# GpSimd adds the two halves of the softmax sums' accumulator, and TensorE multiplies one half with ones

## The chip, the cores and the metric

The kernel runs on one core of a Trainium2 chip. The metric is the device time of one execution in microseconds (us). Each time is the median of several runs; a profile is taken from one further execution, and its span runs from its first to its last instruction.

## What is computed

One layer of a block for 4096 tokens of width 1024. Of the reference, the part that bears on the change is the softmax of sparse attention: 8 query heads over 2 key heads (4 heads a group), 64 wide, where each query sees up to 256 selected keys in earlier chunks of 64:

```python
s = jnp.einsum('bqgrd,bqkgd->bqgrk', qg, kg).astype(jnp.float32) * scale
s = jnp.where(valid[:, :, None, None, :], s, -jnp.inf)
p = jax.nn.softmax(s, axis=-1).astype(v.dtype)
o = jnp.einsum('bqgrk,bqkgd->bqgrd', p, vg)
```

Before it come an RMS norm and one input projection, and the indexer that selects the keys; behind it the gates, two branch products, their sum and the output projection.

## The kernel before

The kernel has four stages, one after the other: norm and projections, the indexer (which leaves for each query block a row of biases, 0 for a selected key and -1e30 for another), the attention, and the output stage. All of the attention works in float32 or float32r (float32 data in a faster mode of TensorE).

The attention runs over 64 units: 32 blocks b of 128 queries, and for each the two key groups g. The text numbers them 0 to 63 in this order, so unit u has b = u // 2. A unit has b + 1 key tiles (kt) of 128 keys, with keys on the partitions and 4 heads x 128 queries on the free axis. For each key tile:

- TensorE computes the logits into a PSUM tile st: two float32r matmuls of 512 columns (L1306, L1307), the second with a row that subtracts the query's maximum.
- VectorE adds the transposed bias bT and writes one half of an SBUF tile tt (L1310); ScalarE takes the exponential in place (L1313). A tile tt holds two key tiles: even ones in half 0, odd ones in half 1.
- TensorE multiplies the exponentials with the values into pv (L1322, `values`), for up to four key tiles at a time, in full float32. Each matmul stands in the trace as two records.
- GpSimd adds each tt to the accumulator acc, both halves in one instruction of 128x1024 (L1337), or half 0 alone, 128x512, if the unit's last key tile has no partner (L1341).

When a unit's key tiles are done, `sums` multiplies acc with a matrix of ones on TensorE and so adds up its 128 partitions (L1355): for each half r of acc and each pair f of heads one float32 matmul of 256 columns, four in all, so eight records. ScalarE copies the result to sm (L1359), SP writes it to DRAM (sumD), reads it back as rl with queries on the partitions (L1368), VectorE takes the reciprocal (L1369), and SP writes it to invD for the output stage. In the last unit the last four tiles tt are not added to acc; the ones multiply them directly.

Beside this, one or two units ahead, TensorE computes the logits of queries on the partitions into ps (L1267), from which VectorE takes the maxima (L1273); they go through DRAM too (maxD, qm). When the last maxima are done, the SP queue starts loading the output stage's weights (raw), which ScalarE and VectorE split into two float32r parts (wb, wa; L235, L237).

The order of instructions on each engine is written by a planner (`Plan`). Every step has an engine, a cost in us, a key, and the steps that it waits for. The planner plays the program through with these costs (and 2.0 us for a DMA to land), lets each engine start the ready step with the lowest key whose buffers are free, and emits the instructions in the order in which they start. It charges 0.12 us more where TensorE changes between float32r and float32 steps. So a cost that changes can move other steps too. On the chip each engine then runs its list in that order, and waits wherever the next instruction isn't ready. Of the buffers, acc has 2, tt 8, st 3, ps 2.

Of the kernel before, what the change touches and what calls it, by code (L numbers as in the profile page):

```python
# [18 lines left out]
OP = mybir.AluOpType  # L19
# [100 lines left out]
class Plan:  # L120
# [11 lines left out]
    def new(self, name):  # L132
        return Tile_(name)
# [107 lines left out]
class K:  # L241
# [890 lines left out]
    def phase_attention(self):  # L1132
# [17 lines left out]
        v, act, pe, gp = nc.vector, nc.scalar, nc.tensor, nc.gpsimd  # L1150
# [18 lines left out]
        pl = Plan()  # L1169
# [116 lines left out]
        def softmax(u):  # L1286
            b, g = units[u]
# [3 lines left out]
            acc, pv, prev, pvs, T, E, done = new("acc"), new("pv"), None, None, {}, {}, 0  # L1291
            direct = DIR if u == len(units) - 1 else 0
            end = at[u + 1]
            runs = -(-(b + 1) // PVN)
            ends = {-(-(b + 1) * (i + 1) // runs) - 1 for i in range(runs)}
            for kt in range(b + 1):
# [18 lines left out]
                if kt in ends:  # L1315
# [3 lines left out]
                    def values(some=some):  # L1319
                        for k in some:  # L1320
                            for f in range(2):
# [3 lines left out]
                                 use=[pv] + [T[q] for q in range(some[0] // 2, kt // 2 + 1)], form=1)  # L1325
                if r == 0 and kt < b:
                    continue
                if p == 0:
                    prev = E[kt]
# [4 lines left out]
                def add(tt=tt, p=p, r=r):  # L1334
# [3 lines left out]
                    else:  # L1338
                        if p == 1:
                            gp.tensor_copy(acc.t[:, 1], first[:, 1])  # L1340
                        gp.tensor_tensor(acc.t[:, 0], first[:, 0], tt.t[:, 0], op=OP.add)  # L1341
                prev = pl.add("pool", 2.3 if r else 1.23, i, add, [prev, E[kt], E[kt - r], E[0], E[1]],
                              [acc] if p == 1 else [], [tt] + ([T[0]] if p == 1 else [acc]))
            ov = new("ov")
            evac = pl.add("act", 0.27, end, lambda: act.activation(ov.t, pv.t, AF.Copy), [pvs], [ov], [pv])
            ps, sm, rl = new("st"), new("sm"), new("rl")

            terms = [(acc if b >= 2 else T[0], min(b + 1, 2))] + [
                (T[p], min(b + 1 - 2 * p, 2)) for p in range(max(1, b // 2 - direct + 1), b // 2 + 1)]

            def sums():
                mine = [(x, r) for x, n in terms for r in range(n)]
                for x, r in mine:
                    for f in range(2):
# [3 lines left out]
                        use=[ps] + [x for x, _ in terms], form=1)  # L1358
# [22 lines left out]
        for b in range(NB):  # L1381
            base = (at[2 * b - 1] if b else 0) - AL - AP
            while first <= b:
                keys(first, base - (b - first) * 1.5)
                first += 1
            queries(b, base)
            flip(b)
            for u in (2 * b, 2 * b + 1):
                maxima(u)
            done = list(pl.steps)  # L1390
            for u in (2 * b, 2 * b + 1):
                softmax(u)
# [182 lines left out]
```

## Time and profile before

| | |
|---|---|
| median of 3 runs | 4342.46 us (4341.94 to 4343.56) |
| profiled execution, its own time | 4339.42 us |
| its span, first to last instruction | 4337.6 us |
| mean granted TensorE clock, share of full | 0.981 |
| TensorE busy | 4176.9 us (96%) |
| VectorE busy | 3226.5 us (74%) |
| ScalarE busy | 2348.8 us (54%) |
| GpSimd busy | 1823.8 us (42%) |

The shares are averages over four stages with different limits. The attention lies between about 2140 and 3600 us of the span; what the change does is read there. In the rows, PE is TensorE, PEld its weight loads, DVE VectorE, ACT ScalarE, POOL GpSimd, and SPq the queue of the engine that issues the DMAs. A number in square brackets behind an instruction is the time that its engine sat idle before it, and the instruction that ended the wait. A stretch in which matmuls overlap counts once as busy; one matmul's duration is longer than the distance to the next one's start.

### The profile page before, as it was taken

The page shows a single profiled execution, that of the slowest core. Times are in us where ns is not written, and L with a number is a line of the kernel's source. Part 1 is how long each engine was busy: PE and PEld are TensorE (multiplying, and loading weights), DVE is VectorE, ACT ScalarE, POOL GpSimd, SP SyncE. Part 2 cuts the span into 40 slices and gives each one's busy share as a digit, 9 for nine tenths or more (in the row PEclk, how much of TensorE's full clock was granted, in tenths as well). Part 3 has the DMA queues.
Part 4 walks back from the last instruction along what each step waited for, and adds up shares of the span by engine and source line. Part 5 has one row for each costly group of instructions (what it writes and reads, how often), then busy time and mean ns, then how long its engine had stood idle before and what let it go on. Part 6 is the DMA issues. An engine that isn't in the chain of part 4 may idle for free. (4 is left out here: it accounts for less than half of the span.)

```text
span 4337.6 us, 77494 instructions
## 1 busy us (share of the span) xinstructions
PE 4176.9 (96%) x27986; PEld 3517.3 (81%) x27987; DVE 3226.5 (74%) x7858; ACT 2348.8 (54%) x3993; POOL 1823.8 (42%) x1657
## 2 busy tenths in 40 slices
PE   8999899999999999999789999999999997999999
PEld 7988899999998999999556666666666656999998
DVE  6545688888989888787578889999999995434342
ACT  5444687777777887886445455555555552111110
POOL 3555222223224332010146678888888881111111
PEclk9999999999999999999799999999999998999999
DMA  6666545545445446666432212212211116444442
GB/s 226 249 235 241 185 161 174 175 173 182 164 166 179 154 159 219 213 220 219 135 65 55 59 44 48 47 47 52 43 38 38 24 27 188 154 135 149 140 141 83
DMA packets 461118, 586.39 MB, mean 135 GB/s; under 512 B 165885, under 2 KB 358969, under 8 KB 456506
## 3 DMA queue, kind: packets, MB, share of 16 engines
q1 hardware_dynamic: 460730, 581.40, 41.4%
q8 instruction: 221, 3.62, 0.4%
q14 instruction: 167, 1.37, 0.1%
HBM read 388.54 MB, written 175.54 MB: 130 GB/s over the span
## 5 line engine op out<-in xcount | busy, mean ns | idle before, releaser
L1043 PE MATMUL pd<-h,wgh 128*128 128x256 f32 x3584 | 1020.4, 285 | 9.7 <-ACT row L417 8.3
L1044 PE MATMUL pd<-h,wgh 128*128 128x256 f32 x3584 | 1013.6, 283 | 0.0
L1045 PE MATMUL pd<-h,wgl 128*128 128x256 f32 x3584 | 1012.7, 283 | 0.0
L1337 POOL TENSOR_TENSOR acc<-acc,tt 128x1024 f32<-128x1024 f32 x388 | 925.7, 2386 | 143.7 <-ACT tt L1313 122.7
L1313 ACT ACTIVATE tt<-tt 128x512 f32<-128x512 f32 x1056 | 653.1, 631 | 601.6 <-DVE tt L1310 599.4
L1310 DVE TENSOR_TENSOR tt<-st,bT 128x512 f32<-128x512 f32 x1056 | 693.8, 684 | 82.5 <-PE st L1307 75.5
L1043 PEld LDWEIGHTS pd<-h,wgh 128*128 128x128 f32 x3584 | 682.1, 190 | 28.2 <-ACT row L417 8.6
L761 DVE SCALAR_TENSOR_TENSOR ring<-rl,wi,ring 128x1024 f32<-128x1024 f32 (+7 forms) x624 | 689.9, 1148 | 12.8 <-ACT rl L759 10.3
L1044 PEld LDWEIGHTS pd<-h,wgh 128*128 128x128 f32 x3584 | 682.9, 191 | 14.9 <-DMA h<-hD 0.2
L1273 DVE CUSTOM_DVE_ANT_0 jk<-ps,bias 128x1024 bf16<-128x1024 f32 (+7 forms) x640 | 655.9, 1028 | 40.2 <-PE ps L1267 39.5
L1045 PEld LDWEIGHTS pd<-h,wgl 128*128 128x128 f32 x3584 | 682.9, 191 | 0.0
L759 ACT ACTIVATE rl<-ps 128x1024 f32<-128x1024 f32 (+7 forms) x624 | 539.4, 889 | 134.2 <-PE ps L756 61.1
L1322 PE MATMUL pv<-tt,vv 128*64 128x256 f32 x4224 | 529.9, 392 | 0.0
L846 ACT ACTIVATE sg<-ring,tk 128x2048 fp8e4<-128x2048 f32 (+7 forms) x322 | 485.4, 1509 | 38.5 <-DVE tk L833 21.2
L1306 PE MATMUL st<-qa,kk 128*128 128x512 f32 x1056 | 455.9, 432 | 18.4 <-DVE tt L1310 18.2
L1322 PEld LDWEIGHTS pv<-tt,vv 128*64 128x64 f32 x4224 | 281.5, 138 | 212.4 <-issue 79.8
L1307 PE MATMUL st<-qm,kl 65*128 65x512 f32 x1056 | 421.6, 399 | 1.1 <-DMA qm<-maxD 1.1
L1267 PE MATMUL ps<-kk,qa 128*128 128x512 f32 (+3 forms) x1152 | 362.7, 391 | 13.7 <-DVE mx L1273 13.7
L1505 POOL TENSOR_TENSOR ga<-ga,gb 128x256 f32<-128x256 f32 x128 | 102.1, 803 | 637.9 <-DVE gb L1500 388.3
L756 PE MATMUL ps<-kis,qT 128*128 128x512 f32 (+3 forms) x1136 | 335.4, 382 | 13.6 <-ACT rl L759 13.4
L1437 ACT ACTIVATE yh<-ga 128x256 fp32r<-128x256 f32 x128 | 53.5, 418 | 517.5 <-PE po L1473 314.2
L1306 PEld LDWEIGHTS st<-qa,kk 128*128 128x128 f32 x1056 | 200.6, 190 | 163.0 <-DVE tt L1310 64.1
(321 smaller groups left out, 7777.4 us busy)
## 6 DMA issues: line engine op xcount, KB each, us to landing
h<-hD SPq DMA_DIRECT2D x192, 1024.0 KB
hlD<-rhl SPq DMA_DIRECT2D x32, 1280.0 KB
gD<-sgm SPq DMA_DIRECT2D x256, 128.0 KB
x<-x SPq DMA_DIRECT2D x32, 512.0 KB
wraw<-w_in SPq DMA_DIRECT2D x32, 512.0 KB
hD<-hh SPq DMA_DIRECT2D x32, 512.0 KB
hD<-hl SPq DMA_DIRECT2D x32, 512.0 KB
q<-hlD SPq DMA_DIRECT2D x32, 512.0 KB
```

Of the source, the lines that this page charges most:

```text
L759: r = pl.add("act", 0.05 + n * 0.834e-3, k_, lambda ps=ps, rl=rl, n=n: act.activation(rl.t[:, :n], ps.t[:, :n], AF.Relu), [m], use=[ps, rl])
L761: prev[o] = pl.add("dve", 0.1 + n * 1.04e-3, k_, lambda rl=rl, o=o, n=n, h=h: v.scalar_tensor_tensor(acc[:, o:o + n], rl.t[:, :n], self.wi ...
L846: mine.append(pl.add("act", 0.28 + m * 0.834e-3, key, lambda sg=sg, o=o, m=m, e=e, j=j, b=b: act.activation(sg.t[:, o:o + m], where[b][:, ...
L1043: pe.matmul(out, wh.t[:, k], r1, start=(k == 0), stop=False)
L1044: pe.matmul(out, wh.t[:, k], r2, start=False, stop=False)
L1045: pe.matmul(out, wl.t[:, k], r1, start=False, stop=(k == KT - 1))
L1273: v.tensor_tensor_reduce(out=jk.t[:, :n], in0=ps.t[:, :n], in1=BI[b][0].t[:, o:o + n], scale=1.0, scalar=-3e38, op0=OP.add, op1=OP.max, ac ...
L1306: pe.matmul(s.t, kk[:, g, o], qa.t[:, hs], start=True, stop=False)
L1310: ad = pl.add("dve", 0.602, i, lambda s=s, tt=tt, r=r, kt=kt: v.tensor_tensor(tt.t[:, r], s.t, bc(bt.t[:, kt:kt + 1], [P, 4, P]), op=OP.ad ...
L1313: E[kt] = pl.add("act", 0.52, i, lambda tt=tt, r=r: act.activation(tt.t[:, r], tt.t[:, r], AF.Exp), [ad], use=[tt])
L1322: pe.matmul(pv.t[64 * f:64 * f + 64], vv[:, k, 64 * g:64 * g + 64], T[k // 2].t[:, k % 2, 2 * f:2 * f + 2], start=(k == 0), stop=(k == b))
L1337: gp.tensor_tensor(acc.t, first, tt.t, op=OP.add)
```

## The change

Each unit with b of 2 or more gets one more GpSimd instruction behind its last add: half 1 of acc is added to half 0, in place (128x512, planned at 1.28 us). The ones then multiply half 0 alone, so `sums` has two matmuls (four records) instead of four. Its planned cost falls by 0.43 us through the count of terms, and it waits for the new add. In the last unit the directly multiplied tiles stay as they were.

```diff
             evac = pl.add("act", 0.27, end, lambda: act.activation(ov.t, pv.t, AF.Copy), [pvs], [ov], [pv])
             ps, sm, rl = new("st"), new("sm"), new("rl")
-
-            terms = [(acc if b >= 2 else T[0], min(b + 1, 2))] + [
+            if b >= 2:
+                prev = pl.add("pool", 1.28, end - 1, lambda: gp.tensor_tensor(
+                    acc.t[:, 0], acc.t[:, 0], acc.t[:, 1], op=OP.add), [prev], use=[acc])
+
+            terms = [(acc, 1) if b >= 2 else (T[0], b + 1)] + [
                 (T[p], min(b + 1 - 2 * p, 2)) for p in range(max(1, b // 2 - direct + 1), b // 2 + 1)]
```

Lines behind this place are three higher in the changed kernel: the ones' line L1355 is L1358 there, the reciprocal's L1369 is L1372, and the new add is L1348.

The planner's order changes as well. Numbers behind a name only tell tiles apart. The first place is GpSimd's list at the end of unit 60 (b = 30, an odd number of key tiles), first before, then after the change.

```order
L1337 TENSOR_TENSOR acc_41140<-acc_41140,tt_41434 128x1024
L1341 TENSOR_TENSOR acc_41140<-acc_41140,tt_41457 128x512
L1337 TENSOR_TENSOR acc_41515<-tt_41475,tt_41495 128x1024
L1337 TENSOR_TENSOR acc_41515<-acc_41515,tt_41519 128x1024
...
L1337 TENSOR_TENSOR acc_41084<-acc_41084,tt_41378 128x1024
L1341 TENSOR_TENSOR acc_41084<-acc_41084,tt_41401 128x512
L1348 TENSOR_TENSOR acc_41084<-acc_41084 128x512
L1337 TENSOR_TENSOR acc_41458<-tt_41419,tt_41439 128x1024
L1337 TENSOR_TENSOR acc_41458<-acc_41458,tt_41467 128x1024
```

The new add (L1348) stands between the unit's last add and the next unit's first.

In the same unit TensorE's list keeps its order, but for the number of ones. On VectorE the reciprocal of this unit's sums moves, counted from the adds of the next unit's logits (L1310): before, then after.

```order
L1310 TENSOR_TENSOR tt_41549<-st_41539,bT_40370 128x512
L1273 ISA jk_41564,mx_41358<-ps_41542,bias_40623 128x1024
L1273 ISA mx_41358 128x1
L1310 TENSOR_TENSOR tt_41571<-st_41546,bT_40370 128x512
L1369 RECIPROCAL rl_41551<-rl_41551 128x4
L1310 TENSOR_TENSOR tt_41571<-st_41568,bT_40370 128x512
...
L1310 TENSOR_TENSOR tt_41492<-st_41481,bT_40320 128x512
L1273 ISA jk_41507,mx_41302<-ps_41485,bias_40569 128x1024
L1273 ISA mx_41302 128x1
L1372 RECIPROCAL rl_41494<-rl_41494 128x4
L1310 TENSOR_TENSOR tt_41515<-st_41489,bT_40320 128x512
L1310 TENSOR_TENSOR tt_41515<-st_41511,bT_40320 128x512
```

The reciprocal now stands one logits add earlier.

The third place is TensorE's list around the sums of unit 47 (b = 23), before and after.

```order
L1267 MATMUL ps_37077<-kk,qa_36542 128x512 x2
L1322 MATMUL pv_36860<-tt_37009,vv 64x256 x4
L1322 MATMUL pv_36860<-tt_37037,vv 64x256 x4
L1355 MATMUL st_37096<-acc_36820,ones 64x256 x4
L1306 MATMUL st_37106<-qa_36542,kk 128x512
...
L1322 MATMUL pv_36810<-tt_36969,vv 64x256 x4
L1322 MATMUL pv_36810<-tt_36999,vv 64x256 x4
L1267 MATMUL ps_37049<-kk,qa_36499 128x512 x2
L1306 MATMUL st_37055<-qa_36499,kk 128x512
L1307 MATMUL st_37055<-qm_36500,kl 128x512
L1267 MATMUL ps_37063<-kk,qa_36499 128x512 x2
L1358 MATMUL st_37068<-acc_36780,ones 64x256 x2
L1306 MATMUL st_37073<-qa_36499,kk 128x512
```

Before, the ones follow the values' matmuls in one group of float32 work; now six float32r matmuls stand between, and the ones are a group of their own. Over the whole attention the float32 groups are 297 before and 308 now.

## Rows read from the trace of the kernel before

**Rows 1.** The page's slices: TensorE's busy share in tenths, 40 slices.

```profile
PE   8999899999999999999789999999999997999999
```

**Rows 2.** Busy times by stretch: us, PE, PEld, DVE, ACT, POOL, clock, DMA.

```profile
2140.00:2500.00 360.00, 335.99 (x1925) 214.79 (x1924) 279.42 (x585) 180.59 (x338) 199.79 (x91) 0.95 0.29 62
2500.00:3526.00 1026.00, 1024.39 (x6062) 682.12 (x6061) 959.10 (x1777) 550.18 (x955) 862.53 (x371) 1.00 0.18 40
3526.00:3605.00 79.00, 53.63 (x320) 30.05 (x319) 54.49 (x77) 38.64 (x80) 41.54 (x18) 0.87 0.25 67
```

**Rows 3.** The chain of waits at unit 60's sums: start us, us, what.

```profile
3464.88 0.86 PE st L1355 x8
```

**Rows 4.** Timeline of TensorE, unit 62: start us, us, what.

```profile
3507.64 1.95 PE L1322 MATMUL pv<-tt,vv 128*64 128x256 f32 x16
...
3510.10 0.64 PE L1267 MATMUL ps<-kk,qa 128*128 128x512 f32 x2
...
3512.22 0.39 PE L1307 MATMUL st<-qm,kl 65*128 65x512 f32 x1
3512.54 1.95 PE L1322 MATMUL pv<-tt,vv 128*64 128x256 f32 x16
```

**Rows 5.** Timeline behind the sums of units 15, 47 and 61.

```profile
2281.48 1.29 DVE L1310 TENSOR_TENSOR tt<-st,bT 128x512 f32<-128x512 f32 x2 [0.48 <-PE st L1307]
...
2999.17 1.03 PE L1355 MATMUL st<-acc,ones 128*64 128x256 f32 x8
3000.14 0.50 PE L1306 MATMUL st<-qa,kk 128*128 128x512 f32 x1
3000.43 2.41 POOL L1337 TENSOR_TENSOR acc<-tt,tt 128x1024 f32<-128x1024 f32 x1 [2.33 <-ACT tt L1313]
3000.97 0.69 DVE L1310 TENSOR_TENSOR tt<-st,bT 128x512 f32<-128x512 f32 x1 [1.28 <-PE st L1307]
...
3505.41 0.69 DVE L1310 TENSOR_TENSOR tt<-st,bT 128x512 f32<-128x512 f32 x1 [0.67 <-PE st L1307]
```

**Rows 6.** GpSimd's half adds (ns min/median/max), and the timeline at units 32 and 61.

```profile
L1341 POOL TENSOR_TENSOR acc<-acc,tt x28: 1272/1289/1295, 2189.1 to 3500.0; 128x512 f32<-128x512 f32 x28
...
2591.17 1.29 POOL L1341 TENSOR_TENSOR acc<-acc,tt 128x512 f32<-128x512 f32 x1
2593.37 1.03 PE L1355 MATMUL st<-acc,ones 128*64 128x256 f32 x8
...
3464.28 2.37 POOL L1337 TENSOR_TENSOR acc<-tt,tt 128x1024 f32<-128x1024 f32 x1 [1.08 <-ACT tt L1313]
```

**Rows 7.** Instructions of lines L1310 and L237: ns min/median/max, first and last start.

```profile
L1310 DVE TENSOR_TENSOR tt<-st,bT x1056: 653/685/694, 2127.2 to 3581.0; 128x512 f32<-128x512 f32 x176
L237 DVE TENSOR_TENSOR wb<-raw,wb x16: 407/1416/2564, 3538.4 to 3574.1; 128x256 fp32r<-128x256 f32 x16
L237 DVE TENSOR_TENSOR wa<-raw,wa x16: 411/425/426, 3579.2 to 3601.6; 128x256 fp32r<-128x256 f32 x16
```

**Rows 8.** Loads of rl and reciprocals (units 29, 60); VectorE's waits, 2500 to 3526.

```profile
2533.88 0.34 SPq L1368 DMA_DIRECT2D rl<-sumD  x1
2535.49 0.18 DVE L1369 RECIPROCAL rl<-rl 128x4 f32<-128x4 f32 x1 [1.26 <-DMA rl<-sumD]
...
3468.28 0.34 SPq L1368 DMA_DIRECT2D rl<-sumD  x1
3471.14 0.17 DVE L1369 RECIPROCAL rl<-rl 128x4 f32<-128x4 f32 x1
...
DVE rl L1369 <- DMA rl<-sumD: 5.0, 6, 1.3
```

**Rows 9.** Timeline of TensorE and SP's queue at the attention's end.

```profile
3584.33 3.62 PE L1355 MATMUL st<-tt,ones 128*64 128x256 f32 x32
3595.62 3.67 SPq L229 DMA_DIRECT2D raw<-w_branch_a  x6
3600.02 0.89 SPq L1449 DMA_DIRECT2D o<-bD  x2
```

## The prediction

> **What bounds the kernel now.** I read the page's slices first: the change acts in slices 20 to 34 of 40, from about 2140 to 3600 us, and TensorE is full in most of them [rows 1]. Next the busy times of stretches, with the granted clock, which is at the upper of its two levels (2.4 GHz) in the middle one [rows 2]. From 2500 to 3526 us, the main stretch, TensorE is busy for 1024.39 of 1026 us, VectorE for 959.10 and GpSimd for 862.53: TensorE sets the pace, with VectorE 6% behind. From 2140 to 2500 TensorE is idle for 24 us, waiting for short units' round trips through DRAM. From 3526 to 3605 it works for 53.63 of 79 us: there the SP queue brings in the branch weights, its last copies start at 3595.62, and only behind them, at 3600.02, does it fetch the output stage's first input, while TensorE has begun its last sums at 3584.33 [rows 9].
>
> Busy time counts overlapping matmuls, so what one takes must be read from starts. The chain of waits puts eight ones records, one unit's sums, at 0.86 us [rows 3]: four take 0.43, and sixteen of the values' matmuls, which have the same shape, 1.72. One cycle of 4.90 us, from the pv group at 3507.64 to the next, holds twelve 512-column float32r matmuls (nine of them, from 3510.10 to 3512.22, take 2.12 us, 0.2356 each: 2.83) and the 1.72 [rows 4]. The 0.35 us that are left are the price of going into a float32 group and out of it.
>
> **What the change removes.** Sixty units (numbers 4 to 63 of 0 to 63, b from 2) go from eight ones records to four: 0.43 us of TensorE each, 25.8 in all. That this time is on the path I read at unit 47 [rows 5]: its sums hold TensorE from 2999.17 to 3000.14, VectorE runs dry and waits 1.28 us for the next logits. The same wait stands 1.7 to 2.0 us behind the start of the sums in each of the 47 units from number 15 (0.48 us) to 61 (0.67), and in 42 of them it is over 0.43 us. So VectorE, which is nearly full, is free just where TensorE gets faster. I count the 34 units of the main stretch (28 to 61) in full: -14.6 us. Of the 24 before 2500 I take three quarters, since round trips hold TensorE up for 7% of that stretch and will take some of the gain back: 24 x 0.43 x 0.75 = -7.7 (bounds 0 and -10.3). The last two units count nothing: the weights' copies end later [rows 9].
>
> **What it adds.** GpSimd gets 60 adds of 128x512. An add of that shape and in place stands in the trace 28 times, at 1.289 us (1.272 to 1.295) [rows 6]: 77 us on an engine that is 16% idle in the main stretch. It goes in behind a unit's last add, where GpSimd waits for the next unit's exponentials anyway: 2.33 us ahead of unit 48 [rows 5], 1.08 ahead of unit 61 [rows 6], and about that at the least in the main stretch. The sums, in order in TensorE's queue with the next unit's logits behind them, must now wait for it. In unit 32 the last add starts at 2591.17, ends 1.29 later and the sums start at 2593.37: 0.91 us between them, less than the new add [rows 6]. But the planner counts 1.28 for the add and moves such sums behind other work (as in unit 47, shown with the change). Where the order stays, the spare time is about 1.4 us or more. Cost: 0; without that cover, up to 0.4 us in a unit.
>
> **What it moves.** By the two orders the float32 groups go from 297 to 308, since sums that shared a group with values now often stand alone: 11 x 0.35 = +3.8 us (bounds 0 and 3.8, as some may stand where TensorE waits anyway). The second move is on VectorE. The reciprocal waits there in order for the sums' round trip through DRAM, and everything behind it waits too. In unit 60 the load of rl is issued at 3468.28 and the reciprocal starts at 3471.14, 2.86 us later, without waiting; the quickest that I find from issue to a reciprocal that did wait is 1.61 us (2533.88 to 2535.49) [rows 8]. The planner now puts the reciprocal one logits add earlier in 12 of the 34 units, counted from the sums, and one later in two. Two adds take 1.29 [rows 5], so the 2.86 us become 2.2: between no wait and 0.6 us each on VectorE, 0 to 7 us. VectorE has idle time behind the sums to make it up, so I take +1.
>
> At the end two more adds of 1.29 us run beside the weights' subtractions. The trace shows what that costs: subtractions with both inputs in SBUF take 1.416 us in the median beside GpSimd's adds (wb, up to 2.564) and 0.425 once these have ended (wa), while the logits' add, which reads PSUM and SBUF, lies between 0.653 and 0.694 throughout [rows 7]. I take +1.3 us (bounds 0 and 2.6, the two adds' whole length). The Trainium skill (SBUF — State Buffer, the section on SBUF's two separate sides) says that VectorE and GpSimd share one port pair, that an instruction holds it to its end, and that a VectorE instruction with two SBUF inputs contends for it. The trace agrees, with 1.416 against 0.425. Read without that condition, as any VectorE instruction against any of GpSimd, the rule would speak against this change in every unit (case 5).
>
> **Sum.** -14.6 - 7.7 + 3.8 + 1.0 + 1.3 = -16.2 us against the profiled execution's own 4339.42: 4323.2. The median of the runs shown is 4342.46, 3.0 above; there it makes 4326.
>
> **The rivals.** (1) The forecast, 4318 to 4333.8: 0.66. (2) All of it: every unit gives its 0.43 us and the new groups cost nothing: 4342.46 - 25.8 = 4317. For it speaks that TensorE is busy to 99.8% of the main stretch; against it that 24 us of waits before 2500 have other causes. 0.10. (3) A wait takes the place of the work removed: VectorE is only 6% behind, and the reciprocals stall it. With 7 us of stalls handed on in full, none of the early units' gain and +2.6 at the end: -14.6 + 3.8 + 7 + 2.6 = -1.2, so 4341; with half the early gain 4337. Against it: the six such waits in the main stretch come to 5.0 us now, and TensorE stays full there [rows 2, 8]. 0.13. (4) Slower: TensorE waits at the sums for the added add. With the whole 1.29 us in sixty units it is +77 - 25.8, so 4394; it decides from a mean wait of 0.27 us in a unit, where 60 x 0.27 equals the sum above. For it: the spare time in unit 32 is shorter than the add. Against it: the planner's price for it is within 0.01 us of the trace's, so it moves what would wait. 0.05. (5) Slower too: GpSimd's adds hold up VectorE's logits adds and maxima by their whole length, +77 less 16: 4403. The 0.694 at most, beside an engine that is 84% busy, speaks against it [rows 2, 7]. 0.02. (6) The sums aren't on the path and nothing changes: 4342. Only the last two units look like that. 0.04.
>
> **The numbers.** A measurement of this kernel can tell about 0.2%, 8.7 us. Faster, under 4333.8: cases 1 and 2 and a little of 3, 0.77. The same, up to 4351: the rest of 3, and 6, 0.16. Slower: 4 and 5, 0.07. The range leaves out the tip of case 2 below (0.05) and, above, 4, 5, 6 and the end of 3 (0.14): 4317 to 4340. The likeliest case's own is 4318 to 4333.8.
>
> **What the profile will show.** If it is right: half of the ones records that read acc, 60 more GpSimd adds at 1.29 us, and VectorE's wait behind the sums shorter by 0.43 in most units, so that the main stretch loses some 12 us and the output stage keeps its length. If case 3: waits of the reciprocal for rl well above 5.0 us in the main stretch, and a TensorE that idles in it. If case 4: the sums' line waits for GpSimd's new line. If the early units, in their new order, lose more in round trips than their 7.7, I am wrong on the slower side.

## The result, and the profile after

The changed kernel takes 4315.05 us (4314.77 to 4317.85, four runs) against 4343.01 (4341.94 to 4343.73, four runs): 28.0 us less, a ratio of 0.9938 [0.9925, 0.9951]. The forecast was 16.2 us less, 4326, with a range down to 4317; the time lies 2 us below the range. So the direction was right, and the gain is larger than the sum by 12 us.

The profiled execution took 4317.85 us. The page's slices of TensorE, one digit for each fortieth of the span, answer to [rows 1]:

```profile
PE   8999899999999999999789999999999997999999
```

The busy times by stretch answer to [rows 2] (us, PE, PEld, DVE, ACT, POOL, clock, DMA share, GB/s):

```profile
2140.00:2500.00 360.00, 331.08 (x1880) 211.40 (x1879) 287.01 (x597) 184.87 (x346) 237.88 (x119) 0.96 0.29 62
2500.00:3500.00 1000.00, 998.62 (x5845) 661.13 (x5844) 945.75 (x1756) 541.50 (x942) 893.46 (x398) 1.00 0.18 42
3500.00:3605.00 105.00, 80.19 (x473) 53.41 (x472) 71.17 (x112) 48.52 (x97) 53.44 (x26) 0.85 0.35 99
```

TensorE is full in the main stretch as before (998.62 of 1000), and GpSimd has gone from 84% to 89% of it. In the first stretch TensorE is idle for 29 us in this execution, where it was 24: work went, and waits did not.

The ones, by line, and below them what TensorE's weight loads waited for there (us, times):

```profile
L1358 PE MATMUL st<-acc,ones x240: 379/379/631, 2165.3 to 3560.5; 128*64 128x256 f32 x120
...
  POOL acc L1348: 1.8, 6
```

The new add, and the time that the reciprocals waited for rl over the whole attention, before and after (us, times):

```profile
L1348 POOL TENSOR_TENSOR acc<-acc x60: 1262/1281/1337, 2158.0 to 3551.6; 128x512 f32<-128x512 f32 x60
```

```profile
  DMA rl<-sumD: 51.8, 29
...
  DMA rl<-sumD: 53.9, 27
```

The ones records that read acc are 240, where they were 480; the 60 adds take 1.281 us each, and the sums wait for them in six places, 1.8 us together. Unit 60 shows both, and the wait behind the sums (start us, us, what, idle before):

```profile
3441.82 1.29 POOL L1341 TENSOR_TENSOR acc<-acc,tt 128x512 f32<-128x512 f32 x1
...
3443.18 1.28 POOL L1348 TENSOR_TENSOR acc<-acc 128x512 f32<-128x512 f32 x1
...
3444.42 2.37 POOL L1337 TENSOR_TENSOR acc<-tt,tt 128x1024 f32<-128x1024 f32 x1
...
3444.62 0.60 PE L1358 MATMUL st<-acc,ones 128*64 128x256 f32 x4
3445.15 0.50 PE L1306 MATMUL st<-qa,kk 128*128 128x512 f32 x1
...
3445.91 0.69 DVE L1310 TENSOR_TENSOR tt<-st,bT 128x512 f32<-128x512 f32 x1 [0.72 <-PE st L1307]
```

From the sums' start to the next logits it is 0.53 us. In the trace before, the same two instructions start 0.97 us apart in this unit, and VectorE's wait behind them was 1.17 us, not 0.72:

```profile
3464.71 1.03 PE L1355 MATMUL st<-acc,ones 128*64 128x256 f32 x8
3465.68 0.51 PE L1306 MATMUL st<-qa,kk 128*128 128x512 f32 x1
...
3466.45 0.69 DVE L1310 TENSOR_TENSOR tt<-st,bT 128x512 f32<-128x512 f32 x1 [1.17 <-PE st L1307]
```

Between the sums of units 28 and 61 VectorE's waits fall, for the logits from 40.5 us (first row, before) to 32.5 and for rl from 5.0 [rows 8] to 3.2 (us in total, times, longest):

```profile
DVE tt L1310 <- PE st L1307: 40.5, 70, 2.1
...
DVE tt L1310 <- PE st L1307: 32.5, 67, 1.3
DVE rl L1372 <- DMA rl<-sumD: 3.2, 3, 1.6
```

Where the time went, read from four starts on the way: TensorE's first ps, the sums of units 28 and 61, and the fetch of the output stage's first input. Before (the fetch, at 3600.02, stands in [rows 9]), then after:

```profile
2115.37 0.65 PE L1267 MATMUL ps<-kk,qa 128*128 128x128 f32 x2
...
2507.08 1.03 PE L1355 MATMUL st<-acc,ones 128*64 128x256 f32 x8
...
3503.66 1.03 PE L1355 MATMUL st<-acc,ones 128*64 128x256 f32 x8
...
2113.40 0.65 PE L1267 MATMUL ps<-kk,qa 128*128 128x128 f32 x2
...
2498.04 0.60 PE L1358 MATMUL st<-acc,ones 128*64 128x256 f32 x4
...
3483.13 0.60 PE L1358 MATMUL st<-acc,ones 128*64 128x256 f32 x4
...
3575.73 0.89 SPq L1452 DMA_DIRECT2D o<-bD  x2
```

So the early stretch (first ps to unit 28's sums) is 384.6 us long, where it was 391.7; the main one (to unit 61's sums) 985.1 for 996.6; the tail (to the fetch) 92.6 for 96.4; and the output stage 740.4 for 737.6. That is -7.1, -11.5, -3.8 and +2.8, and with the 2.0 us that the attention began sooner, -21.6, the difference of the two profiled executions. Another execution of the same program (below) has 376.9 in the early stretch, 7.7 us less; 4.7 of that lies between the sums of units 2 and 3, where the change adds and removes nothing (b = 1). This stretch scatters by several us, and the profiled execution here is the slowest of the four.

### The profile page after: what moved, and what is told of

It reads as the page before. It is cut to its first block, busy times and chain, and to the rows that moved or that the text cites. A ratio compares the mean times of both kernels' runs of the same rounds, so it can differ in the third digit from the quotient of the medians.

```text
span 4316.1 us, 77051 instructions
## 1 busy us (share of the span) xinstructions
PE 4154.3 (96%) x27746; PEld 3497.2 (81%) x27747; DVE 3223.0 (75%) x7858; ACT 2347.8 (54%) x3993; POOL 1904.1 (44%) x1717
## 5 line engine op out<-in xcount | busy, mean ns | idle before, releaser
L1337 POOL TENSOR_TENSOR acc<-acc,tt 128x1024 f32<-128x1024 f32 x388 | 925.5, 2385 | 114.0 <-ACT tt L1313 92.5
L1310 DVE TENSOR_TENSOR tt<-st,bT 128x512 f32<-128x512 f32 x1056 | 694.0, 685 | 65.8 <-PE st L1307 60.0
L1306 PE MATMUL st<-qa,kk 128*128 128x512 f32 x1056 | 456.2, 432 | 15.9 <-DVE tt L1310 14.6
L756 PE MATMUL ps<-kis,qT 128*128 128x512 f32 (+3 forms) x1136 | 335.1, 382 | 13.3 <-ACT rl L759 13.2
```

The lines of the kernel that those rows point to most:

```text
L1306: pe.matmul(s.t, kk[:, g, o], qa.t[:, hs], start=True, stop=False)
L1310: ad = pl.add("dve", 0.602, i, lambda s=s, tt=tt, r=r, kt=kt: v.tensor_tensor(tt.t[:, r], s.t, bc(bt.t[:, kt:kt + 1], [P, 4, P]), op=OP.ad ...
L1337: gp.tensor_tensor(acc.t, first, tt.t, op=OP.add)
```

## The experiments

The theory that I started from after the result: the removed work gives about what the sum says, and the rest comes from the planner's new order, which the prediction had counted as a cost only. The rivals: the first profile misled and the time is nearer the forecast; the work alone gives all of it; GpSimd's add costs something that the waits don't show.

Times are medians, with the lowest and highest. Differences are against the kernel before in the same batch (4339.45 for the first four, 4338.71 for the next four, 4339.63 for the last four; its own single runs spread from 4329.45 to 4347.94).

| run | us | ratio [95%] | difference |
|---|---|---|---|
| e1_after_again | 4312.91 (4310.01 to 4313.69) | 0.9935 [0.9921, 0.9948] | -26.5 |
| e2_work_only | 4316.30 (4311.79 to 4319.45) | 0.9942 [0.9929, 0.9956] | -23.2 |
| e3_order_only | 4326.59 (4325.59 to 4329.48) | 0.9970 [0.9957, 0.9982] | -12.9 |
| e4_no_add | 4315.72 (4311.58 to 4318.48) | 0.9942 [0.9928, 0.9955] | -23.7 |
| e5_cost_26 | 4330.62 (4326.35 to 4333.14) | 0.9983 [0.9974, 0.9992] | -8.1 |
| e6_before_fe6 | 4323.09 (4321.20 to 4324.94) | 0.9964 [0.9950, 0.9977] | -15.6 |
| e7_after_fe6 | 4297.24 (4293.25 to 4298.30) | 0.9901 [0.9886, 0.9916] | -41.5 |
| e8_after_land3 | 4297.56 (4296.35 to 4299.14) | 0.9906 [0.9891, 0.9921] | -41.2 |
| e9_order_early | 4331.41 (4322.72 to 4334.17) | 0.9979 [0.9970, 0.9988] | -8.2 |
| e10_order_main | 4341.62 (4337.20 to 4350.12) | 1.0004 [0.9994, 1.0013] | +2.0 |
| e11_order_tail | 4337.18 (4333.63 to 4343.30) | 0.9992 [0.9983, 1.0001] | -2.5 |
| e12_land3_fe6 | 4307.17 (4304.75 to 4311.43) | 0.9923 [0.9910, 0.9937] | -32.5 |

The stretches of each run's profile, cut at the same four starts, with TensorE's idle time in the early one (its length less TensorE's busy time in it):

| run | early | idle in it | main | tail | output stage |
|---|---|---|---|---|---|
| before | 391.7 | 27.5 | 996.6 | 96.4 | 737.6 |
| after | 384.6 | 33.4 | 985.1 | 92.6 | 740.4 |
| e1 | 376.9 | 27.8 | 985.1 | 93.9 | 741.5 |
| e2 work only | 382.4 | 29.1 | 984.1 | 94.1 | 741.0 |
| e3 order only | 379.2 | 19.2 | 1001.4 | 92.6 | 735.5 |
| e4 no add | 380.6 | 28.6 | 982.7 | 96.3 | 743.3 |
| e5 | 379.5 | 24.1 | 996.9 | 95.4 | 738.1 |
| e6 | 376.8 | 18.2 | 996.0 | 96.2 | 739.0 |
| e7 | 365.6 | 19.3 | 985.5 | 92.5 | 738.7 |
| e8 | 360.0 | 16.2 | 984.2 | 90.5 | 747.2 |
| e9 | 378.4 | 20.1 | 997.3 | 95.2 | 740.0 |
| e10 | 391.4 | 27.9 | 998.5 | 95.1 | 738.6 |
| e11 | 392.6 | 30.3 | 998.6 | 95.3 | 735.9 |
| e12 | 365.6 | 19.6 | 984.5 | 90.5 | 747.3 |

**The changed kernel again (e1).** Nothing is edited.

> The changed kernel once more, unaltered, to see how much of its gain repeats. If single executions scatter and the first measurement was lucky, the gain falls to 22 us or less, as the two profiles show (4339.42 and 4317.85, 21.6 apart). If the gain is a property of the kernel, it stays at 28 us, within 2.

It came to -26.5 us: the gain stands in another batch, and is some 10 us over the sum. The rival that the first measurement misled falls. By the table this profile lies 14.8 us under the one of before in the early stretch, 11.5 in the main one and 2.5 in the tail, and 3.9 over it in the output stage.

**The work without the order (e2).** The new add is planned at no cost and the sums at their old one, so that each engine's list is that of before, but for the 60 adds and the halved ones:

```diff
-                prev = pl.add("pool", 1.28, end - 1, lambda: gp.tensor_tensor(
+                prev = pl.add("pool", 0.0, end - 1, lambda: gp.tensor_tensor(
...
-            s1 = pl.add("pe", 0.43 * sum(n for _, n in terms), end + FD, sums, [prev, E[b], pvs],
+            s1 = pl.add("pe", 0.43 * (sum(n for _, n in terms) + (b >= 2)), end + FD, sums, [prev, E[b], pvs],
```

> The work of the change in the order of the kernel before: the added GpSimd instruction and the two ones matmuls that are left are issued, but the planner is told a cost of 0 for the add and the old cost of the sums, so that every engine's list stands as before but for these. Theory A (the work on TensorE is what counts, and the new order costs 3.8 us for its 11 groups and 1 for the reciprocals): -14.6 - 7.7 + 1.3 = -21 us, or -25 if the early units give all of theirs, so faster than the changed kernel's forecast by some 5. Theory B (the new order gave what the forecast lacked): less than 20 us, clearly slower than the changed kernel. If the add makes TensorE wait where the order no longer makes room for it (unit 32 by 0.4, some others by 0.1 to 0.3), 1 to 3 us less.

It gave -23.2 of the 25.8 us that the removed work comes to, so it lies where theory A put it and speaks against B. Between the sums of units 28 and 61 it takes off 12.5 us; 0.43 for each of the 33 units there would be 14.2. The sums do wait for the add in this order, as this row of their line shows (us, times):

```profile
  POOL acc L1348: 8.2, 15
```

With the planner's order it is 1.8 in six places. So the planner's move of the sums does what the prediction said of it, though these 8.2 us are mostly bought back elsewhere, as e4 shows.

**The order without the work (e3).** The other half: before's instructions, in the order that the planner makes with the new costs. A step that emits nothing stands in for the add.

```diff
+            if b >= 2:
+                prev = pl.add("pool", 1.28, end - 1, lambda: None, [prev], use=[acc])
...
-            s1 = pl.add("pe", 0.43 * sum(n for _, n in terms), end + FD, sums, [prev, E[b], pvs],
+            s1 = pl.add("pe", 0.43 * (sum(n for _, n in terms) - (b >= 2)), end + FD, sums, [prev, E[b], pvs],
```

> The order of the changed kernel with the work of the one before: all four ones matmuls and no added GpSimd instruction, but planned as if there were one, and two. Theory A: +3.8 for the 11 new float32 groups and +1 for the reciprocals: 3 to 6 us slower than before. Theory B: faster than before by 5 us or more, by the order alone.

The order alone is worth -12.9 us, as theory B has it, where the prediction had it as a cost. Its profile puts the gain in the early stretch (379.2 for 391.7, with 8.3 us less idle time on TensorE) and in the tail (92.6 for 96.4), and a loss in the main one (1001.4 for 996.6). The two halves make 36.1 us together, and the whole change 26.5 in this batch, so some 10 us are claimed by both. Single places show it: from the sums of unit 21 to those of unit 22 the work alone takes off 3.3 us, the order alone 2.7, and both together 2.6 and 2.7 in the two executions of the changed kernel; from unit 26 to 27 it is 2.6, 6.2 and, together, 6.7.

In the main stretch the changed kernel and e3 have the same order, and there the changed kernel is faster by 0.35 to 0.48 us in 31 of the 33 distances from one unit's sums to the next. So the 0.43 us are on TensorE's path there, unit by unit, as the prediction said. Of the 4.8 us by which e3 is longer than before, 3.2 stand at one place, from unit 29 to 30, where a reciprocal waits 2.73 us for rl; in the other three profiles with this order there (after, e1, e10) it waits 1.35 to 1.60, and the distance is longer by 0.2 at the most. The other 32 distances come to +1.6.

**The work without the add (e4).** As e2, but GpSimd adds nothing; the odd key tiles' exponentials are missing from the sums (a constant of 1e-6 keeps them above zero).

```diff
-            if b >= 2:
-                prev = pl.add("pool", 1.28, end - 1, lambda: gp.tensor_tensor(
-                    acc.t[:, 0], acc.t[:, 0], acc.t[:, 1], op=OP.add), [prev], use=[acc])
```

> The order of the kernel before, the ones matmuls for the even half only, and no added GpSimd instruction: the odd key tiles are left out of the sums (a constant of 1e-6 is added where ScalarE copies them, so that the reciprocal is of something). Against the run with the work in the old order it prices the add alone. Theory A: the add costs 1.3 us at the end and nothing else, so the two agree within 2. Rival: the add costs by making TensorE wait for the sums or by holding up VectorE: then this one is faster by over 4 us.

The time is 0.6 us under e2's, less than either's spread: theory A. Sixty adds, 77 us of GpSimd, cost TensorE nothing that can be told, though in e2 the sums wait for them 15 times; in the main stretch it is 1.4 us (984.1 and 982.7).

**One swap in SP's list (e5).** Set beside e3's, the trace of before loses most at two places, units 12 and 26, some 6 us at each (5.7 from unit 12's sums to the next, 6.2 from unit 26's); I took the second. There SP issues (start us, us, what), in the kernel before, and VectorE and TensorE follow:

```profile
2460.41 0.58 SPq L1281 DMA_DIRECT2D maxD<-mf  x1
2461.04 0.59 SPq L1366 DMA_DIRECT2D sumD<-sm  x2
2463.53 0.68 SPq L1282 DMA_DIRECT2D qm<-maxD  x1
2464.32 1.18 SPq L1368 DMA_DIRECT2D rl<-sumD  x1
...
2468.07 0.18 DVE L1369 RECIPROCAL rl<-rl 128x4 f32<-128x4 f32 x1 [3.79 <-DMA rl<-sumD]
2468.88 0.80 PE L1306 MATMUL st<-qa,kk 128*128 128x512 f32 x1 [3.28 <-DVE tt L1310]
```

The store of another unit's maxima (maxD) stands ahead of that of the sums, and their load (qm), which must wait for it to land, ahead of the load of rl. VectorE, in order, stands still at the reciprocal for 3.79 us, and TensorE, out of logits tiles that VectorE has emptied, for 3.28. The four microseconds of that wait and the twelve behind it, in stretches of 4 us (columns as in [rows 2]):

```profile
2464.00:2468.00 4.00, 1.59 (x10) 1.20 (x8) 0.27 (x1) 0.63 (x1) 1.96 (x1) 1.00 0.09 1
2468.00:2472.00 4.00, 3.12 (x12) 2.33 (x14) 3.94 (x7) 1.71 (x5) 2.37 (x1) 0.54 0.23 44
2472.00:2476.00 4.00, 4.00 (x21) 2.30 (x18) 0.81 (x3) 1.93 (x5) 2.29 (x2) 0.61 0.07 22
2476.00:2480.00 4.00, 4.00 (x26) 2.49 (x25) 3.93 (x7) 2.98 (x6) 2.17 (x2) 1.00 0.61 158
```

Behind the idle time the granted clock is near the lower of its two levels (1.2 GHz, 0.50 of full) for most of 8 us. By these rows that costs another 3.0 us, as an estimate, each busy time multiplied by what the clock lacks of full: 3.12 x 0.46 + 4.00 x 0.39. With the 3.28 it makes 6.3 for one late load. To test this place by itself I changed only the planned cost of unit 26's sums in the kernel before; it swaps SP's stores and loads there:

```diff
-            s1 = pl.add("pe", 0.43 * sum(n for _, n in terms), end + FD, sums, [prev, E[b], pvs],
+            s1 = pl.add("pe", 0.43 * (sum(n for _, n in terms) - (u in (26,))), end + FD, sums, [prev, E[b], pvs],
```

> The kernel before, with one planned number changed: the sums of unit 26 are planned at 0.43 us instead of 0.86. All the work stays. In the SP queue this moves unit 26's store of the sums ahead of the maxima's store, and its load of rl ahead of the load of qm, as the changed kernel's order does; elsewhere a handful of instructions near that place trade places. Theory C (the new order gained where it moved the sums' round trip ahead of the maxima's in the SP queue, so that the reciprocal no longer holds up VectorE): 4 to 7 us faster by this one swap, and VectorE's wait of 3.79 us at unit 26's reciprocal is gone. Rival (the gain of the order came from TensorE's list): 0, within 2.

SP's list and the reciprocal at that place in e5:

```profile
2455.95 0.74 SPq L1366 DMA_DIRECT2D sumD<-sm  x2
2456.73 0.35 SPq L1281 DMA_DIRECT2D maxD<-mf  x1
2457.59 1.09 SPq L1368 DMA_DIRECT2D rl<-sumD  x1
2459.36 0.68 SPq L1282 DMA_DIRECT2D qm<-maxD  x1
...
2460.05 0.18 DVE L1369 RECIPROCAL rl<-rl 128x4 f32<-128x4 f32 x1 [0.28 <-DMA rl<-sumD]
```

The wait of 3.79 us is 0.28, and the same two stretches of 4 us are granted the full clock:

```profile
2459.50:2463.50 4.00, 4.00 (x26) 2.60 (x24) 3.72 (x8) 2.85 (x6) 3.86 (x2) 1.00 0.22 7
2463.50:2467.50 4.00, 4.00 (x26) 3.09 (x26) 3.45 (x7) 3.10 (x7) 2.90 (x2) 1.00 0.60 169
```

The sums of units 26 and 27 start 19.00 us apart (2453.39 and 2472.39), where it was 25.23 (2457.90 and 2483.13): -6.2, as the estimate has it, and the next pair gives another 2.1. The time falls by 8.1 us [0.9974, 0.9992], a little over the 4 to 7 expected. VectorE's reciprocals stand where they stood. One pair of DMAs in another order, with no work removed, is worth about a third of the change. The changed kernel's list has the same order there, and its two sums stand 18.56 apart (2454.74 and 2473.30).

**The other place, unit 12.** No run changes this place alone, but the traces show that it is another case. First before, then e3, behind sums that start at 2238.95 and 2239.00:

```profile
2246.01 1.17 SPq L1368 DMA_DIRECT2D rl<-sumD  x1
2250.19 0.18 DVE L1369 RECIPROCAL rl<-rl 128x4 f32<-128x4 f32 x1 [4.69 <-DMA rl<-sumD]
2251.20 0.47 PE L1267 MATMUL ps<-kk,qa 128*128 128x128 f32 x1 [3.75 <-DVE mx L1273]
...
2247.77 0.52 SPq L1370 DMA_DIRECT2D rl<-sumD  x1
2250.41 0.18 DVE L1371 RECIPROCAL rl<-rl 128x4 f32<-128x4 f32 x1 [2.88 <-DMA rl<-sumD]
2251.82 0.73 PE L1267 MATMUL ps<-kk,qa 128*128 128x512 f32 x2 [1.27 <-DVE mx L1273]
```

The sums' store and load stand behind the maxima's in both, and in e3 the load of rl is issued even later; the reciprocal starts as late, 11.4 us behind the sums for 11.2. But on VectorE it stands two logits adds later, so that VectorE and TensorE have more to do meanwhile. The granted clock from 2248 to 2256 is 0.73 and 0.50 in the two stretches of 4 us before, and 1.00 in e3. e6, below, moves this reciprocal by the same two adds with the same four transfers in the same order on SP, and gains 6.0 us there.

**Later reciprocals (e6, e7).** `FE` is the number of key tiles by which a reciprocal's key lies behind its unit's other late steps. Six for two gives the round trip more time ahead of VectorE's next wait, in the kernel before (e6) and in the changed one (e7):

```diff
-FE = 2
+FE = 6
```

> The kernel before, with the reciprocal planned 6 key tiles behind its sums instead of 2; the SP queue and TensorE keep their order but for a few places. Theory C: VectorE's 51 us of waits for rl mostly go, and with them the part of the early units' stalls that they cause: 5 to 15 us faster. Rival (VectorE's waits for rl cost nothing, as it has idle time): 0, within 2.

> The changed kernel with the reciprocal planned 6 key tiles behind its sums. Theory C: VectorE's waits for rl, 53 us in the changed kernel, mostly go, and it gets 5 to 12 us faster than the changed kernel, so 32 to 40 faster than before. Rival: no difference to the changed kernel.

e6 takes 15.6 us off the kernel before, nearly all of it in the early stretch (376.8 for 391.7). VectorE's waits for rl fall less than I had thought, from 51.8 us over the attention to the first of these rows, e6's; the second is e7's, for 53.9 in the changed kernel.

```profile
  DMA rl<-sumD: 39.4, 20
```

```profile
  DMA rl<-sumD: 27.7, 15
```

TensorE's idle time in the early stretch falls by 9.3 us in e6, to 18.2. From e6 to e7 the change is worth 25.9 us, much as without the later reciprocals (26.5 in e1), and these are worth 15.6 and 15.0: these two gains add. e7, at -41.5, is a little faster than the 32 to 40 expected. That 25.9 is 60 x 0.43 = 25.8 is partly chance: the early stretch gives 11.2 of it (376.8 to 365.6), where the work of 24 units is 10.3, the main one 10.5, where 33 are 14.2, and the tail 3.7, where the prediction counted nothing. No run has the work alone with the later reciprocals, so how much of the 25.9 is order isn't shown.

**A longer landing in the plan (e8, e12).** The planner counts 2.0 us for a DMA to land; here 3.0, in the attention of the changed kernel. In e12 `FE` is 6 as well.

```diff
-                    d.ready = max(d.ready, now + (2.0 if s.eng == "dma" else lat if d.eng != s.eng else 0.0))
+                    d.ready = max(d.ready, now + (self.land if s.eng == "dma" else lat if d.eng != s.eng else 0.0))
...
         pl = Plan()
+        pl.land = 3.0
```

> The changed kernel, planned with 3.0 us instead of 2.0 from a DMA's issue to its landing in the attention; the trace shows 1.6 to 3.9 for the loads of rl. Theory C: the planner then moves the reciprocals and the loads of qm to where they don't wait, in all round trips: 5 to 12 us faster than the changed kernel. Rival: the order only changes by chance, and the time by less than 4 either way.

> The changed kernel with both repairs of the plan: 3.0 us for a DMA's landing, and the reciprocal 6 key tiles behind its sums. If each takes away the same waits: no faster than either alone, some 41 us under the kernel before. If each reaches waits that the other leaves (27 and 16 us of VectorE's waits for rl remain in the two): 3 to 8 us more.

e8 is as fast as e7, by the same stretch (360.0), and beats the 5 to 12 expected. Together they are worse than either, by 9 us, which neither expectation had: of e8's gain in the early stretch 5.6 us are lost, and 3.1 lie ahead of the attention, where no edit reaches. Both runs with 3.0 have an output stage of 747 us, some 4 us or more above all others; their traces put it in its first 75 us, where TensorE is busy for 54 us at a granted clock of 0.80 and 0.78, for 61 at 0.85 in the trace before. What causes that was not tried. e7 and e8 are the best versions here, some 15 us under the changed kernel of e1 by their differences in their own batches.

**The order by parts (e9 to e11).** As e3, but with the new costs for some units alone: 4 to 27 (e9), 28 to 61 (e10), 62 and 63 (e11). Of e9, for the others alike:

```diff
+            if 2 <= b and u < 28:
+                prev = pl.add("pool", 1.28, end - 1, lambda: None, [prev], use=[acc])
...
-            s1 = pl.add("pe", 0.43 * sum(n for _, n in terms), end + FD, sums, [prev, E[b], pvs],
+            s1 = pl.add("pe", 0.43 * (sum(n for _, n in terms) - (2 <= b and u < 28)), end + FD, sums, [prev, E[b], pvs],
```

> The work of the kernel before; only units 4 to 27 are planned as in the changed kernel (the add at 1.28 us that is never issued, the sums at 0.43), so that the order changes in the early stretch alone. Theory C (the order gains through the round trips of the short units): 9 to 13 us faster, with unit 28's sums that much earlier. Rival (the order gains elsewhere, or evenly): under 5 us.

> The same for units 28 to 61 alone: 9 more float32 groups on TensorE (306 for 297), the work as before. By the price of a group that the forecast read from one cycle, 0.35 us: 3.2 us slower, and up to 1 more by the reciprocals. Rival (a group that stands alone costs TensorE less, since it waits there anyway): within 1.5 of before.

> The same for units 62 and 63 alone. In the profiles the time from unit 61's sums to the output stage's first fetch is 96.4 us before and 92.6 with the new order. If the order of the last two units makes this: 3 to 4 us faster. Rival (it comes from what lies ahead): within 1.

The early units hold the gain, -8.2 [0.9970, 0.9988], a little under the 9 to 13 expected; its profile has 13.3 less in the early stretch, 12.4 of them at units 12 and 26, and 2.7 more ahead of the attention. The main ones lose 2.0, which their interval doesn't tell from nothing, nor from the 3.2 expected. The profile tells more: e10's main stretch is 1.9 us longer, and its distances from sums to sums differ from e3's by less than 0.1 us in 32 of 33; without unit 29's they come to +1.7, for e3's +1.6. So the order does cost the main stretch some 1.6 us. (e11's main stretch, planned as before, is 2.0 longer too, but 2.2 of that stands at one place, from unit 49 to 50.) The tail's -2.5 is not told from nothing either. The three sum to -8.7, e3 gave -12.9; the intervals of four measurements cover that.

## Why the prediction was off

**The step that failed is "What it moves".** It counted the planner's new order as two costs, +3.8 for float32 groups and +1.0 for earlier reciprocals, nearly all in the main stretch. Of the early one it asked only how much of the removed work waits would take back, though [rows 2] had shown TensorE idle for 24 us behind round trips there; that the order might shorten these waits it put at nothing, without a reason. The order alone is worth -12.9 us (e3), -8.2 by the early units alone (e9). Behind the removed work it is -3.3 (from e2 to e1, which their intervals don't tell from nothing; the forecast's +4.8 is out, as e1's five runs are all under e2's median). By this sum the work gave 2 us more than its forecast (-14.6 - 7.7 + 1.3 = -21.0 for -23.2), and the order 8 us more (+4.8 for -3.3).

What the runs showed in its place are two long waits of VectorE for rl. At unit 26 the new order puts the store and load of the sums ahead of another unit's load of its maxima on SP's queue; that by itself is 6.2 us there (e5). At unit 12 the reciprocal stands two logits adds later on VectorE, and 5.7 to 6.2 us are gone (e3, e9); that this is the cause is supported by e6 but not tested alone. The prediction did not compare SP's list, and counted VectorE's reciprocals in the main stretch only; in the early one, by the same count, six stand earlier and four later.

**What the change removes** was sized nearly right in sum. The work alone gives -23.2 (e2) and -23.7 (e4), against a forecast of -22.3 before costs. In the main stretch it is -12.5 (e2) and -13.9 (e4), against -14.6; in the early one -9.3 (e2) and -11.1 (e4), against -7.7. The reason for three quarters, that round trips take some of the gain back, does not show with the old order, but with the new one: there TensorE's idle time goes up from e3's 19.2 us to 27.8 and 33.4 in the changed kernel's two executions. Removed work and better order draw in part on the same waits, so the two gains don't add.

**GpSimd's add costs nothing**, as forecast: 0.6 us between e2 and e4, and 1.8 us of waits in six places. It ran at 1.281 us; 1.289 was expected [rows 6].

**The float32 groups and the reciprocals** were forecast at +4.8 us together, nearly all in the main stretch. With the work gone, the new order costs 1.0 us there (985.1 in both executions of the changed kernel, 984.1 in e2); with the work as before it costs some 1.6, in e3 and e10 alike, and once 3.2 more by a late load of rl. Nine new groups at 0.35 us [rows 4] would be 3.2, so the two terms were two to three times too large; how the 1.6 us divide between groups and reciprocals isn't shown. The changed kernel's waits for rl in the main stretch went from 5.0 to 3.2 us. The forecast for the main stretch, "some 12 us", came out at 11.5.

**The tail** was forecast at +1.3 and came out at -3.8 and -2.5 in two executions. The price of the contention was read rightly: wb's subtractions take 1.390 us in the median beside GpSimd's adds and wa's 0.424 without them, as in [rows 7], and the logits' add stays between 0.658 and 0.695.

```profile
L237 DVE TENSOR_TENSOR wb<-raw,wb x16: 409/1390/2005, 3517.6 to 3552.3; 128x256 fp32r<-128x256 f32 x16
L237 DVE TENSOR_TENSOR wa<-raw,wa x16: 406/424/426, 3554.3 to 3577.3; 128x256 fp32r<-128x256 f32 x16
```

That is again as the Trainium skill has it (SBUF — State Buffer, the section on SBUF's two separate sides): a VectorE instruction with two SBUF inputs contends with a GpSimd instruction that reads SBUF, and one with at most one SBUF input, like the logits' add, does not, outside of certain modes. But the stretch got shorter, not longer. It is 95.1 to 96.4 us in the runs whose last units are as before (e6, e9 and e10 among them) and 94.1 and 96.3 where only work is taken away (e2, e4), while e3, with the new order alone, has 92.6. So the order seems to shorten it; e11, meant to show that, has 95.3 and didn't settle it, and why stays open.

**The output stage** was to keep its length. It is 740.4 and 741.5 us in the two executions of the changed kernel, and 741.0 and 743.3 in e2 and e4, against 735.5 to 740.0 in the seven runs with all the ones' work. But e7 has 738.7, so it isn't settled that the change does this, and its cause was not tried.

**The rivals.** Case 2 named the time, 4317, within 2 us, but not the cause: the work alone does not give it, and the groups are not free. Case 3's waits of the reciprocal exist, in the early stretch and before the change as much as after it (51.8 and 53.9 us). Case 4 is there with 1.8 us, far from its 0.27 us a unit. Case 5 is out by the logits' add, case 6 by e2. The case that came was not on the list: that the new order shortens waits of the early units for rl. That 4317 is so near is luck: it takes all of the work and nothing of the order.

## What to carry to other kernels

When a change of costs makes a planner write a new order, the order is a change by itself: read the lists where the trace of before shows its longest waits, those of the DMA queue and of the engine that waits first, and count what may go away there as well as what may come. A wait of an engine whose clock falls when it idles costs more than its length: 3.28 us of idle time cost 6.2 here. And two gains that draw on the same wait don't add; measure each half alone, and compare the halves place by place.

## What had not been expected of the hardware

The granted clock was 0.54 and 0.61 in the two stretches of 4 us behind an idle time of 3.28 us, and 1.00 before it and from 2476 on; the first two matmuls of 512 columns behind a group of values start 0.59 us apart there (2474.11 and 2474.70) and 0.34 apart at the full clock (2463.67 and 2464.01). The load of rl took 3.75 us from issue to reciprocal behind the load of qm (2464.32 to 2468.07) and 2.46 ahead of it in e5; how much of that is the queue and how much the landing was not taken apart. Single runs of the kernel before lie between 4329 and 4348 us, and two executions of the changed kernel differ by 7.7 us in the early stretch alone, with the same lists on every engine, while their main stretches are 985.1 both. Where engines wait for round trips through DRAM, one profile gave a stretch to some 8 us only.
